# A two-layer hybrid trunk on one core: the framework's scheduler orders the queues by a timeline simulation instead of its default estimates

## The chip, the core and the metric

The kernel runs on one core of a Trainium2 chip. The core has five engines that run their own queues of instructions: TensorE (PE, with its weight loads shown as PEld), VectorE (DVE), ScalarE (ACT), GpSimd (POOL) and SyncE (SP), which here issues all DMAs. An engine takes its instructions strictly in the order of its queue, and an instruction waits on semaphores that other engines or landed DMAs raise. The metric is the device time of one execution in microseconds, from three runs and one profiled execution.

## The reference

A trunk of two layers works on 1024 latent tokens and 256 context tokens of width 1024, in fp32. Each layer modulates its input (adaLN), projects it, mixes it by two groups of heads, gates, projects out, and normalises the residual.

```python
# layer 0
oa = block_attention(qa, concat([ka_c, ka], 1), concat([va_c, va], 1))   # MLA heads
ob = block_attention(qb, concat([kb_c, kb], 1), concat([vb_c, vb], 1))   # GQA heads
y  = concat([oa * silu(ga), ob * silu(gb)], -1) @ w_out
# layer 1, per direction: gated DeltaNet in chunks of 64, and RG-LRU
sol = triangular_solve(I + M, rhs, lower=True, unit_diagonal=True); u, w = split(sol)
v_new = u - w @ s;  o = qd @ s + attn @ v_new;  s = s * gl + kd^T @ v_new     # scan over chunks
h = linear_scan(a, b, h0)                                                      # RG-LRU
# both layers
x = layer_norm(alpha * x + gate * y)
```

## The kernel before, in words

Every fp32 product is made of three matmuls on parts of the operands: a high part in a reduced format and the rest (names ending in h and l: wh/wl, hh/hl, qh/ql). The splits are made by ScalarE, VectorE and GpSimd. Tokens are worked in tiles of 128, and two column ranges of a wide product run in PSUM tiles of 512 columns.

The stages in order of time: modulation and input projection of layer 0 (to about 360 us); attention with its softmax sums, GQA heads first and MLA heads after (to about 880); the output projection and normalisation, tile by tile (to about 1060); the input projection of layer 1 with the RG-LRU's convolutions and scans beside it (to about 1300); the preparation of the DeltaNet (to about 1510), its triangular levels, scan and output projection (to the end).

What matters here of the attention: score matmuls read the query tiles qh and ql, which have two buffers each and are loaded from d_q (lines 683 and 684). While the GQA heads run, the weights of the MLA heads are fetched in pieces into tiles f with three buffers (lines 639 and 652) and split into wukv and wuq by ScalarE and GpSimd. GpSimd also adds the softmax terms (accp).

What matters of the DeltaNet's preparation: for each tile of tokens VectorE writes decayed products into two tiles WX, one for each direction, and SyncE stores them to d_w (line 1758) and d_xa (line 1760). When five tiles are stored, the 32x32 blocks on their diagonals are loaded (line 1785, tiles ia) and inverted by a chain of 30 steps with two instructions each: direction 0 on VectorE, direction 1 on GpSimd. The result is stored to d_bu (line 1802), its transpose (tile it) to d_bt (line 1805):

```python
eng = nc.gpsimd if dr else nc.vector
...
eng.tensor_tensor(tv, A[:, rows, j].unsqueeze(2).broadcast_to([80, nr, ncl]),
                  A[:, j, cols].unsqueeze(1).broadcast_to([80, nr, ncl]), op=ALU.mult)
eng.tensor_tensor(A[:, rows, cols], A[:, rows, cols], tv, op=ALU.add)
...
nc.sync.dma_start(d["bu"][dr, ...], A)
T = self.til(gp, [80, 32, 32], F32, "it", bufs=1)
eng.tensor_copy(T, A.rearrange("p a b -> p b a"))
nc.sync.dma_start(d["bt"][dr, ...], T)
```

There are four inverses: ia_2716 and ia_2816 on VectorE, ia_2717 and ia_2817 on GpSimd. The levels and the scan load W, X, Tt, Tu, K and V (lines 1839 to 1859) from what was stored. Beside the preparation run convolutions (tiles yc), weight splits (wf) and the projections of the gates, whose PSUM tiles are emptied through tiles tm.

Two things set the order of the work. The first is the kernel's own planner (class Core, lines 93 to 110): it counts a cost for every instruction that is emitted and lets generators of background work emit when an engine's count is behind TensorE's. It fixes the order in which the instructions are emitted. The second is the framework's scheduler, which runs when the tile context closes. It gives every engine a queue: of the instructions that its own estimates of time make ready it takes the one emitted first. It also gives tiles their buffers and sets the waits. Almost all compute instructions are recorded with line 88, since they go through one helper; the names of the tiles tell them apart.

## Time and profile before

| | us |
|---|---|
| three timed runs | 1791.7, 1804.87, 1804.99 |
| median | 1804.87 |
| profiled execution | 1793.42 |
| its span, first to last instruction | 1791.6 |
| TensorE busy in it | 1636.8 |
| VectorE, ScalarE, GpSimd busy | 1169.4, 738.1, 798.5 |
| mean granted clock of TensorE, as a share of full speed | 0.957 |
| data moved by DMA | 234.31 MB |

The profile is that of one execution. A row of its timeline gives the start in us from the beginning of the span, the duration in us, engine and line, operation, output and inputs by the program's names, shapes, how many such instructions in a row are put together, and, in brackets, how long the engine stood idle before the row and what it waited for.

### The profile page before, as it was taken

What the parts mean: (1) busy time and instruction counts of PE and PEld (TensorE: products, weight loads), DVE (VectorE), ACT (ScalarE), POOL (GpSimd) and SP (SyncE); (2) the same over time, 40 slices, a digit from 0 to 9 for tenths busy, and PEclk for the clock granted to TensorE, in tenths of its full rate; (3) what the DMA queues carried; (4) which work ended last, traced back from release to release, by engine and by line L of the source; (5) the groups of instructions that cost most, each with busy time, mean ns of one, the idle gap of its engine ahead of it and who ended that gap; (6) DMA issues with size and microseconds to landing.
All of it is one profiled execution on the core that took longest, in us unless ns stands there. A gap on an engine that the chain in (4) does not pass through costs nothing.

```text
span 1791.6 us, 25469 instructions
## 1 busy us (share of the span) xinstructions
PE 1636.8 (91%) x9020; PEld 1196.4 (67%) x9020; DVE 1169.4 (65%) x2186; ACT 738.1 (41%) x1498; POOL 798.5 (45%) x727
## 2 busy tenths in 40 slices
PE   5999999988999999999899989979978958899997
PEld 2997776744555665656467877756855747799885
DVE  2757713235667767666847976998846596477786
ACT  2533401144554554544524445767733312233431
POOL 1432200066657778767642752322204483573120
PEclk8999999998999999999899999989988979899999
DMA  7343396155231101011243323333456637897542
GB/s 304 114 142 118 120 315 202 66 127 157 66 84 48 51 21 47 28 55 54 89 124 105 119 91 118 106 120 121 124 153 167 155 107 219 280 250 229 183 159 94
DMA packets 239931, 234.31 MB, mean 131 GB/s; under 512 B 61958, under 2 KB 188306, under 8 KB 237756
## 3 DMA queue, kind: packets, MB, share of 16 engines
q1 hardware_dynamic: 239804, 232.69, 42.4%
q8 instruction: 71, 1.16, 0.3%
q14 instruction: 56, 0.46, 0.1%
HBM read 162.97 MB, written 69.66 MB: 130 GB/s over the span
## 4 chain that ended last, share of the span: by engine, by line
PE 57%; DVE 18%; issue 7%; DMA 6%; POOL 5%; ACT 4%; SPq 2%; DVEq 0%; ACTq 0%; POOLq 0%
PE ps L88 39%; PE pb L88 10%; PE pv L88 8%; DVE yc L88 3%; DVE f L88 2%; DVE mx L88 1%; DVE ia L88 1%; DVE itmp L88 1%; POOL ia L88 1%; DMA modw<-in_mod_w 1%; POOL itmp L88 1%; DVE nsq L88 1%; DVE lu L88 1%; POOL lu L88 1%; DMA wst<-in_att_w_in 1%
## 5 line engine op out<-in xcount | busy, mean ns | idle before, releaser
L88 DVE TENSOR_REDUCE mx<-ps 128x1 f32<-128x512 f32 (+1 forms) x384 | 206.9, 593 | 161.3 <-PE ps L88 160.2
L88 POOL TENSOR_TENSOR accp<-accp,pt 128x512 f32<-128x512 f32 x202 | 266.1, 1340 | 71.0 <-ACT pt L88 69.4
L88 PE MATMUL ps<-h1h,wf 128*128 128x512 f32 (+1 forms) x864 | 276.7, 394 | 5.7 <-DVE tm L88 3.5
L88 ACT ACTIVATE pt<-pb 128x512 f32<-128x512 f32 (+1 forms) x352 | 194.7, 577 | 194.8 <-PE pb L88 191.1
L88 PE MATMUL pb<-qh,kb 96*128 96x512 f32 (+4 forms) x528 | 209.1, 411 | 1.7 <-ACT pt L88 1.2
L88 PEld LDWEIGHTS ps<-h1h,wf 128*128 128x128 f32 x864 | 164.0, 196 | 41.9 <-issue 5.6
L88 PE MATMUL ps<-h1l,wf 128*128 128x512 f32 (+1 forms) x432 | 164.7, 381 | 0.0
L88 PEld LDWEIGHTS pb<-qh,kb 128*128 128x128 f32 (+2 forms) x528 | 99.9, 191 | 88.9 <-issue 66.2
L88 PE MATMUL pb<-ql,kb 66*128 66x512 f32 (+3 forms) x352 | 136.8, 389 | 0.0
L88 PE MATMUL ps<-kb,qh 128*128 128x512 f32 (+3 forms) x416 | 120.5, 365 | 13.3 <-DMA qh<-d_q 9.7
L88 POOL TENSOR_TENSOR accp<-pt,pt 128x512 f32<-128x512 f32 (+1 forms) x47 | 54.2, 1171 | 140.5 <-ACT pt L88 128.5
L88 PEld LDWEIGHTS ps<-kb,qh 128*128 128x128 f32 (+1 forms) x416 | 75.9, 189 | 48.9 <-DMA qh<-d_q 10.3
L88 DVE SCALAR_TENSOR_TENSOR yc<-xb,rT,yc 128x1283 f32<-128x1283 f32 (+1 forms) x48 | 88.8, 1859 | 26.2 <-ACT yc L88 25.9
L88 POOL TENSOR_TENSOR ml<-m,mh 128x512 fp32r<-128x512 f32 (+1 forms) x24 | 45.5, 1908 | 116.4 <-ACT mh L88 107.1
L88 PEld LDWEIGHTS ps<-h1l,wf 128*128 128x128 f32 x432 | 85.0, 197 | 16.5 <-issue 3.7
L88 PE MATMUL ps<-wl,hh 128*128 128x416 f32 (+2 forms) x240 | 83.6, 348 | 7.6 <-DVE wl L88 3.8
L88 PE MATMUL ps<-wh,hh 128*128 128x416 f32 (+2 forms) x240 | 83.9, 349 | 3.8 <-ACT wh L88 2.7
L88 PE MATMUL pv<-pt,vm 128*64 128x512 f32 (+1 forms) x352 | 83.0, 589 | 4.1 <-DVE mo L88 2.7
L88 PE MATMUL ps<-wo,mh 128*128 128x512 f32 x256 | 83.0, 403 | 2.4 <-ACT wo L88 2.2
L88 PE MATMUL pv<-pt,vgqa 128*64 128x512 f32 (+1 forms) x352 | 84.2, 600 | 1.0 <-DVE mo L88 1.0
L88 PE MATMUL ps<-wh,hl 128*128 128x416 f32 (+2 forms) x240 | 82.7, 345 | 0.1
L88 PE MATMUL ps<-w,mh 128*128 128x512 f32 x256 | 81.3, 398 | 0.0
(373 smaller groups left out, 3679.9 us busy)
## 6 DMA issues: line engine op xcount, KB each, us to landing
modw<-in_mod_w SPq DMA_DIRECT2D x16, 1024.0 KB
wfs<-in_rec_w_in SPq DMA_DIRECT2D x22, 512.0 KB
modw<-in_mod_w SPq DMA_DIRECT2D x16, 512.0 KB
wst<-in_att_w_in SPq DMA_DIRECT2D x24, 256.0 KB
d_q<-qo SPq DMA_DIRECT2D x20, 256.0 KB
lx<-d_xl SPq DMA_DIRECT2D x8, 640.0 KB
d_w<-WX SPq DMA_DIRECT2D x20, 256.0 KB
W<-d_w SPq DMA_DIRECT2D x20, 256.0 KB
```

The costliest lines, as they stand in the source:

```text
L88: return fn(*args, **kw)
```

## The change

One argument is added where the tile context is opened.

```diff
-    with tile.TileContext(nc) as tc:
+    with tile.TileContext(nc, schedule_with_timeline_sim=True) as tc:
         Trunk(tc, I, out).run()
```

The scheduler then takes the times at which instructions become ready from a simulation of the engines' timelines, and no longer from its default estimates. The instructions are emitted as before. Both programs have the same 7592 matmuls and 884 DMAs, and the same compute instructions on the other engines but for 31 loads of ScalarE's function tables instead of 29; only their order in each queue differs, and which buffer a tile gets. No matmul is moved by more than 51 places, and in the attention the orders of TensorE and VectorE are the same.

Place 1 is SyncE's queue at the end of the first half of the GQA heads, with the load of the query tiles qh_807 and ql_808. Before:

```order
L875 DMA d_mix_17_94<-mo_712_3502 128x256
L639 DMA f_773_3688<-in_mla_w_ukv 128x4x64
L639 DMA f_789_3747<-in_mla_w_ukv 128x4x64
L627 DMA mlat_734_3561<-in_k_mla 128x1024
...
L639 DMA f_803_3800<-in_mla_w_ukv 128x4x64
L683 DMA qh_807_3818<-d_q12_12_89 128x4x128
L684 DMA ql_808_3819<-d_q12_12_89 64x4x128
```

and with the change:

```order
L639 DMA f_757_3631<-in_mla_w_ukv 128x4x64
L639 DMA f_773_3688<-in_mla_w_ukv 128x4x64
...
L875 DMA d_mix_17_94<-mo_712_3502 128x256
L639 DMA f_789_3747<-in_mla_w_ukv 128x4x64
L639 DMA f_803_3800<-in_mla_w_ukv 128x4x64
L652 DMA f_824_3859<-in_mla_w_uq 128x4x96
L683 DMA qh_807_3818<-d_q12_12_89 128x4x128
L684 DMA ql_808_3819<-d_q12_12_89 64x4x128
```

The piece f_803 needs the buffer of f_757, which is free when GpSimd has made wukv of it; f_824 needs that of f_773. On GpSimd this first wukv row stands now behind accp of pt_746, 12 places earlier than before, where it stood behind accp of pt_814; the second one follows two rows after it.

Place 2 is SyncE's queue near the end of the DeltaNet's preparation. Before, the store d_bu of GpSimd's first inverse (ia_2717) and that of its transpose stand ahead of the stores of two pairs of WX tiles:

```order
L1760 DMA d_xa_2189_8715<-WX_2766_11988 512x1x128
L1802 DMA d_bu_2191_8717<-ia_2717_11798 80x1024
L1805 DMA d_bt_2190_8716<-it_2840_12356 80x1024
L1572 DMA d_v_2182_8708<-tm_2827_12282 128x4x128
L1758 DMA d_w_2188_8714<-WX_2790_12113 128x4x128
L1760 DMA d_xa_2189_8715<-WX_2790_12113 512x1x128
...
L1758 DMA d_w_2188_8714<-WX_2809_12194 128x4x128
...
L1785 DMA ia_2816_12224<-d_w_2188_8714 20x32x32 x4
L1785 DMA ia_2817_12229<-d_w_2188_8714 20x32x32 x4
```

With the change:

```order
L1758 DMA d_w_2188_8714<-WX_2790_12113 128x4x128
...
L1758 DMA d_w_2188_8714<-WX_2809_12194 128x4x128
L1760 DMA d_xa_2189_8715<-WX_2809_12194 512x1x128
L1758 DMA d_w_2188_8714<-WX_2810_12195 128x4x128
L1760 DMA d_xa_2189_8715<-WX_2810_12195 512x1x128
L1785 DMA ia_2816_12224<-d_w_2188_8714 20x32x32 x4
...
L1802 DMA d_bu_2191_8717<-ia_2717_11798 80x1024
...
L1785 DMA ia_2817_12229<-d_w_2188_8714 20x32x32 x4
L1805 DMA d_bt_2190_8716<-it_2840_12356 80x1024
```

The WX stores and the loads for VectorE's second inverse stand ahead of d_bu now; those for GpSimd's second inverse stay behind it. On VectorE the rows of WX_2809 and WX_2810 follow those of WX_2790 and WX_2791 directly, where one wf row and two yc_2830 rows stood between them. Further on, the row that empties the PSUM tile of the z gate (tm_2873) stood behind 42 rows of the second inverse, and stands behind 11 of them now.

Place 3 is TensorE's queue in the input projection of layer 0, where two PSUM tiles (ps_220 and ps_221) are summed over the pieces of one weight. Before, one after the other:

```order
L88 MATMUL ps_220_970<-wl_205_923,hh_23_106 128x256
L88 MATMUL ps_220_970<-wh_204_922,hl_24_107 128x256
L88 MATMUL ps_221_997<-wh_183_880,hh_23_106 128x256
L88 MATMUL ps_221_997<-wl_184_881,hh_23_106 128x256
L88 MATMUL ps_221_997<-wh_183_880,hl_24_107 128x256
```

With the change, mixed:

```order
L88 MATMUL ps_221_997<-wl_184_881,hh_23_106 128x256
L88 MATMUL ps_221_997<-wh_183_880,hl_24_107 128x256
L88 MATMUL ps_221_997<-wh_186_886,hh_23_106 128x256
L88 MATMUL ps_220_970<-wh_198_910,hh_23_106 128x256
L88 MATMUL ps_221_997<-wl_187_887,hh_23_106 128x256
```

The matmuls of the second tile with the early pieces stand between those of the first tile with the late pieces. The same is done at two more places: with the next weight, and at the end of the attention, where matmuls of the context's output projection (pb_2174, pb_2175) now precede those of the last softmax sum.

## Rows read from the trace of the kernel before

**Rows 1.** The page, part 1: busy us, share of the span, instructions of each engine.

```profile
PE 1636.8 (91%) x9020; PEld 1196.4 (67%) x9020; DVE 1169.4 (65%) x2186; ACT 738.1 (41%) x1498; POOL 798.5 (45%) x727
```

**Rows 2.** Stretches: us, busy PE, PEld, DVE, ACT, POOL (instructions), clock, DMA share, GB/s.

```profile
0.00:50.00 50.00, 30.61 (x152) 15.55 (x153) 15.55 (x34) 13.60 (x27) 8.84 (x14) 0.86 0.82 313
...
1430.00:1515.00 85.00, 61.11 (x281) 49.23 (x280) 72.29 (x139) 19.99 (x43) 51.33 (x75) 0.84 0.55 158
1515.00:1575.00 60.00, 52.16 (x634) 44.16 (x634) 26.53 (x71) 15.28 (x40) 35.74 (x57) 0.89 0.89 274
1575.00:1690.00 115.00, 110.84 (x1400) 102.41 (x1397) 86.77 (x257) 47.09 (x133) 50.63 (x79) 0.99 0.77 231
...
1440.00:1466.00 26.00, 7.70 (x22) 5.32 (x21) 24.97 (x40) 2.36 (x7) 23.33 (x35) 0.55 0.25 59
```

**Rows 3.** Timeline of TensorE, 416 to 433 us.

```profile
416.97 0.40 PE L88 MATMUL pb<-qh,kb 128*128 128x512 f32 x1
...
432.40 0.79 PE L88 MATMUL ps<-kb,qh 128*128 128x512 f32 x1 [8.37 <-DMA qh<-d_q]
```

**Rows 4.** Waits of SyncE's queue, 405-434 and 1385-1420 us: total, times, longest.

```profile
SPq L639 <- POOL wukv L88: 19.1, 1, 19.1
...
SPq L1802 <- POOL ia L88: 15.8, 1, 15.8
```

**Rows 5.** Timeline of SyncE's queue in the same two stretches.

```profile
428.86 0.38 SPq L639 DMA_DIRECT2D f<-in_mla_w_ukv  x1
429.35 0.45 SPq L683 DMA_DIRECT2D qh<-d_q  x1
...
1409.79 0.87 SPq L1758 DMA_DIRECT2D d_w<-WX  x1
```

**Rows 6.** Timeline of VectorE, 1414 to 1501 us.

```profile
1414.40 0.88 DVE L88 SCALAR_TENSOR_TENSOR WX<-ps,g_s,D 128x256 f32<-128x256 f32 x2 [12.26 <-DMA d_xa<-WX]
...
1432.90 0.68 DVE L88 TENSOR_SCALAR ia<-ia 80x1024 f32<-80x1024 f32 x1
...
1499.92 1.13 DVE L88 COPY it<-ia 80x1024 f32<-80x1024 f32 x1
```

**Rows 7.** Timeline of GpSimd, 1430 to 1476 us.

```profile
1430.14 2.77 POOL L88 TENSOR_SCALAR ia<-ia 80x1024 f32<-80x1024 f32 x1 [21.27 <-DMA ia<-d_w]
...
1473.85 2.16 POOL L88 COPY it<-ia 80x1024 f32<-80x1024 f32 x1
```

**Rows 8.** Chain of waits before 1513 us: start, us, what.

```profile
1507.73 5.29 DMA Tt<-d_bt
```

**Rows 9.** Timeline of TensorE, 1457 to 1514 us.

```profile
1457.87 0.69 PE L88 MATMUL ps<-ident,yc 128*128 128x128 f32 x2 [17.35 <-DVE tm L88]
...
1513.11 0.64 PE L88 MATMUL ps<-Tt,W 32*32 32x32 f32 x16 [1.86 <-DMA Tt<-d_bt]
```

**Rows 10.** Timeline of VectorE: two products of the inverse of one size.

```profile
1444.76 0.77 DVE L88 TENSOR_TENSOR itmp<-ia 80x234 f32<-80x234 f32 x1
...
1481.75 0.40 DVE L88 TENSOR_TENSOR itmp<-ia 80x234 f32<-80x234 f32 x1
```

**Rows 11.** Timeline of TensorE: three shorter waits in layer 0.

```profile
102.95 0.39 PE L88 MATMUL ps<-wl,hh 128*128 128x256 f32 x1 [2.42 <-POOL wl L88]
...
145.98 0.79 PE L88 MATMUL ps<-wl,hh 128*128 128x512 f32 x1 [2.95 <-DVE wl L88]
...
885.58 1.16 PE L88 MATMUL pv<-pt,vm 128*64 128x256 f32 x8 [2.71 <-DVE mo L88]
```

**Rows 12.** Timeline of TensorE, first loads of the scan.

```profile
1544.55 3.35 PE L88 MATMUL ps<-V,Lt 128*128 128x128 f32 x16 [3.01 <-DMA V<-d_v]
...
1561.19 0.80 PE L88 MATMUL ps<-K,L 128*128 128x128 f32 x2 [4.62 <-POOL K L88]
```

**Rows 13.** The page, part 5: a group | busy us, mean ns | idle before, releaser.

```profile
L88 DVE SCALAR_TENSOR_TENSOR yc<-xb,rT,yc 128x1283 f32<-128x1283 f32 (+1 forms) x48 | 88.8, 1859 | 26.2 <-ACT yc L88 25.9
```

**Rows 14.** Groups of ScalarE, in the same columns.

```profile
L88 ACT ACT_TABLE_LOAD x29 | 37.2, 1283 | 13.6 <-DVE yc L88 12.4 <-PEq L2229 0.7
```

## The prediction, made before the changed kernel was run

> **What bounds the kernel now.** I read the engine totals first: TensorE is busy 91% of the span [rows 1], so time can only be won where it stands still or where it runs slowly. I then cut the span into stages [rows 2]: in the stage 1430 to 1515 TensorE works 61.11 of 85 us at a granted clock of 0.84 while VectorE works 72.29; in 1515 to 1575 the DMA engines are 89% busy; in 1575 to 1690 TensorE works 110.84 of 115, so hardly anything is to be had there. Last I listed TensorE's waits. The two longest are 8.37 us at 432.40 [rows 3] and 17.35 us at 1457.87 [rows 9]. Neither is a shortage of an engine: behind each, SyncE's queue stands at one DMA whose data is late, while DMAs that are ready stand behind it [rows 4, 5]. The change gives every engine's queue another order, so I followed both programs through these two places and through the smaller waits.
>
> **Base of the sum.** The profiled execution took 1793.42 us (span 1791.6). The timed runs are 1791.7, 1804.87 and 1804.99: two groups 12 us apart, and the trace belongs to the lower. I make the sum against 1793.42 and let the range carry the other group.
>
> **Term 1, the query load at 432: -8 us.** Before, SyncE holds the third mla_w_ukv load group's last piece (L639) until GpSimd has split the first one, a wait of 19.1 us [rows 4], and issues it at 428.86; the query loads (L683, L684) stand behind it and start at 429.35 [rows 5]. TensorE starts with them at 432.40, so a load needs 3.05 us from issue to use. The buffer they fill is read for the last time by the score matmul at 416.97 [rows 3]. In the change GpSimd splits that weight 12 places earlier, among accp sums, so SyncE gets past it and waits for the buffer alone: issue about 417.5, usable about 420.5. TensorE arrives at 432.40 - 8.37 = 424.03, so the wait goes. Late next is nothing that I can see: TensorE's order around it is the same, and 8.3 of 8.37 should stay, since TensorE is what limits the attention stage. Bounds: -8.4, and 0 if another load in front (L652, which now precedes the query loads) is as late as L639 is now. I take -8, since its split is only two GpSimd rows further on.
>
> **Term 2, the inverses at 1390 to 1513: -9 us.** Before, SyncE waits 15.8 us at L1802 for the end of GpSimd's inverse [rows 4], then for its transpose (L1805), and the stores of the ready WX tiles (L1758, L1760) leave only at 1409.79 [rows 5]. The next WX has no buffer until they land: VectorE stands 12.26 us, until 1414.40 [rows 6]. Everything after hangs on that: GpSimd's second inverse starts at 1430.14 after 21.27 us of idling [rows 7], VectorE's at 1432.90, and the latter ends with the copy at 1499.92 [rows 6]; its transposed result is stored, loaded (5.29 us) and only then do TensorE's triangular levels run on, at 1513 [rows 8, 9]. The change puts both pairs of WX stores and the four block loads of VectorE's inverse ahead of L1802, so VectorE need not stand at 1402. It takes one wf subtraction and two yc passes after the WX instead of before, which costs nothing in sum, and then meets the block loads. Now the last of eight pieces is there 1430.14 - 1414.40 = 15.7 us after the first WX row [rows 6, 7]; the four that VectorE needs should be there in two thirds of it, 10 us. Until it needs them it has the WX, some 3 us, and four rows of the yc kind, of 1.86 us or less [rows 13], 7 us. That is nearly even; I leave up to 3 us of new wait: 12.26 - 3 = 9 us gained at the end of its chain, and from there at 1513.
>
> What of TensorE's 17.35 us? It waits for the evacuation tm, which stands on VectorE behind 42 rows of the inverse; in the change 11 rows precede it, so this wait should go, and with it the slow clock behind it: granted 0.55 in 1440 to 1466 [rows 2]. But TensorE then only arrives earlier at the levels, which wait for VectorE's chain. The wait moves there; it is no gain of its own. Bounds: 0 (all given back at 1513) and -20 (the 17.35 and some 2.5 of slow clock, if VectorE's chain were not the end). I take the value that VectorE's row gives.
>
> **Term 3, small fillings: -4 us.** TensorE waits 2.42 us at 102.95 and 2.95 at 145.98 for weight splits, and 2.71 at 885.58 at the last softmax sums [rows 11]. In the change matmuls of another accumulation, whose operands are there, stand in front of the waiting ones. Of the 8.1 us I count half, since the producers (GpSimd and VectorE) set the pace of the following tile too. Bounds: -8.1 and 0.
>
> **Term 4, start: +1 us.** SyncE's queue begins with eight 1 MB modw loads and the context rows; now six weight pieces of 0.2 MB and the rotary tables of 0.26 MB stand among them, 1.5 MB, which at the 313 GB/s of this stage [rows 2] bring the context rows 4.8 us later. TensorE gets the same pieces back as smaller waits for weights, for which it stands now and then up to 50. I take most of it as given back. Bounds: -1, +4.8.
>
> **Term 5, the scan's loads: -2 us.** TensorE waits 3.01 us for V and 4.62 for K [rows 12]. The V loads move ahead of the kk/qq loads, and one w_out load of 256 KB leaves the way of K. Against it three 512 KB broadcasts move from the scan's last third to the crowded stretch. At that stage's 274 GB/s [rows 2] these 1.5 MB are 5.7 us of DMA. Bounds: -7.6, +6.
>
> **Term 6, ScalarE's tables: 0.** 31 instead of 29 loads of 1.283 us [rows 14] are 2.6 us on an engine that is busy 41%. TensorE's nearest matmuls cover it; uncovered it costs 2.6.
>
> **Allowance: +5 us.** 230 of 7592 matmuls and 275 VectorE rows stand elsewhere; new waits can't be read from the old trace. I allow two of the size of those in [rows 11].
>
> Sum: -8 - 9 - 4 + 1 - 2 + 0 + 5 = -17, so 1793.4 - 17 = 1776 us.
>
> **A rule that speaks against term 2.** VectorE's inverse rows are slower while GpSimd's inverse runs: the 80x234 product takes 0.77 us at 1444.76, and 0.40 at 1481.75, after GpSimd's chain has ended [rows 7, 10]. The Trainium skill, "SBUF — State Buffer", section "SBUF: two separate sides", says that VectorE and GpSimd share a port pair as an exclusive lock, which a VectorE operation with two SBUF inputs and a GpSimd operation can't hold together, so one blocks. The trace agrees with it in those two rows; carried as far as in rival (a) it makes the time 1783 instead of 1776.
>
> **Rivals.**
> (a) *The two inverses hinder each other more.* GpSimd's chain lasts from 1430.14 to 1476.0, 46 us; each of them costs VectorE 1 - 0.40/0.77 = 0.48 us of work. If more VectorE work of other kinds falls opposite it and stretches it by a third, 15 us, VectorE loses 7 and term 2 is -2: 1783. For it: both chains slide together, with yc passes now between the inverse's rows. Against it: the work displaced then runs after GpSimd's end, at 0.40. Chance 0.18.
> (b) *TensorE's wait is itself the path.* If the levels' loads come early enough, term 2 is -20: 1765. Against it: the chain of waits runs over VectorE's copy and the Tt load. Chance 0.12.
> (c) *Slower: the scan's loads fall behind.* Ten steps from 1540 to 1690 each need K, X and V from one queue. If in the new order a load that waits for a buffer (w_out's wait for VectorE's split of the one before) stands in front of them, a K comes late in each step by about 3 us, the V wait of [rows 12]: 10 x 3 = 30 us, and 1776 + 2 + 30 = 1808, later than before. It decides where a K lands after the state of the step before is done, for which TensorE's 4 us of slack in 1575 to 1690 is the measure [rows 2]. Against it: for every step the K and V loads have the same buffer wait as before and follow it at once. Chance 0.08.
> (d) *It does not do what the orders show:* SyncE is held at both places by some other late operand, and the rest cancels: 1793. Chance 0.12.
> The forecast keeps 0.50.
>
> **How the numbers follow.** The forecast's own range, from the bounds of its terms, is 1766 to 1787 (the bounds of terms 1 to 5 don't all come together). Rivals (a) and (b) lie in it or at its edge. If the runs fall in the upper group it is 1777 to 1798. The range 1760 to 1799 takes these in with most of (d), and leaves out (c). The median before is 1804.87, and 1% (about what a measurement can tell) is 18 us: below 1786.8 counts as faster. In the lower group the forecast, (b) and most of (a) are, in the upper one (b) and half of the forecast; like against like the gain is just under 1%. I give faster 0.50, same 0.43, slower 0.07, the last for (c) and what I can't see.
>
> **What would show it.** Right: no wait of TensorE over 1 us near 424 and the L683 issue at about 417; SyncE's wait for GpSimd's inverse no longer in front of a WX store, and no VectorE wait of 12 us near 1400; the tm evacuation less than 2 us after TensorE needs it; a TensorE wait for Tt of over 10 us that has taken its place; the Tt matmuls of 1513 at about 1493 (-8 - 9 - 4 + 1). Wrong: inverse rows on VectorE at 0.7 us and more over most of the chain (a); waits for K or X over 2 us in several steps of the scan (c); a new SyncE wait over 10 us with query or WX DMAs behind it (d).

## The result, and the profile after

The changed kernel takes **1790.35 us** (median of ten runs, 1785.47 to 1794.67). The kernel before, in ten runs, takes 1800.31 us (1791.70 to 1804.99). The ratio is 0.994 with a 95% interval of 0.9921 to 0.9959: about 10 us faster, which is clear of the noise and less than the 1% from which on the forecast counted a change as faster. The forecast was 17 us faster and 1776 us. Of the 14 us between 1776 and 1790, 7 are the base: the ten runs of before don't form two groups, as I had read the three that I saw, and the profiled execution of 1793.42 lies 6.9 us under their median. The other 7 are the effect itself, and the rest of this text is about them. (One of the five runs of s5_both_back below took 1941.35 us at a granted clock of 0.786; its ratio leaves it out.)

The profiled execution after took 1786.52 us, its span is 1784.7. The totals that answer to [rows 1]:

```profile
PE 1630.5 (91%) x9020; PEld 1195.9 (67%) x9020; DVE 1177.7 (66%) x2186; ACT 741.0 (42%) x1500; POOL 811.2 (45%) x727
```

TensorE is 6.3 us less busy with the same matmuls (less of it at the slow clock), VectorE 8.3 and GpSimd 12.7 us busier with the same instructions. So the rows of these two engines take longer in sum; one such row is followed below.

**The query load.** SyncE's queue and then TensorE, timeline, at the place of [rows 3, 5] (columns: start, length, engine, line, operation, and in brackets the idle time before it with what ended it):

```profile
406.05 4.93 SPq L652 DMA_DIRECT2D f<-in_mla_w_uq  x1
414.70 0.37 SPq L683 DMA_DIRECT2D qh<-d_q  x1
```

```profile
422.06 0.51 PE L88 MATMUL ps<-kb,qh 128*128 128x512 f32 x1
```

The load leaves at 414.70 instead of 429.35, and the score matmul that waited 8.37 us starts at 422.06 without a bracket, so without a wait. L652, which now stands in front of the load, is through at 410.98; after it the load waits 3.9 us more for its buffer, which TensorE still reads.

**The inverses.** Their places of [rows 4 to 10]: SyncE, VectorE and TensorE after the change.

```profile
1394.40 0.37 SPq L1758 DMA_DIRECT2D d_w<-WX  x1
1396.81 3.43 SPq L1785 DMA_DIRECT2D ia<-d_w  x4
1408.85 0.33 SPq L1802 DMA_DIRECT2D d_bu<-ia  x1
```

```profile
1389.94 0.88 DVE L88 SCALAR_TENSOR_TENSOR WX<-ps,g_s,D 128x256 f32<-128x256 f32 x2 [2.98 <-DMA d_xa<-WX]
1392.32 2.44 DVE L88 SCALAR_TENSOR_TENSOR WX<-ps,g_s,D 128x256 f32<-128x256 f32 x6 [1.50 <-DMA d_xa<-WX]
...
1402.53 0.69 DVE L88 TENSOR_SCALAR ia<-ia 80x1024 f32<-80x1024 f32 x1 [1.36 <-DMA ia<-d_w]
...
1422.59 0.39 DVE L88 TENSOR_TENSOR itmp<-ia 80x234 f32<-80x234 f32 x1
...
1486.15 1.03 DVE L88 COPY it<-ia 80x1024 f32<-80x1024 f32 x1
```

```profile
1497.16 0.64 PE L88 MATMUL ps<-Tt,W 32*32 32x32 f32 x16 [19.50 <-DMA Tt<-d_bt]
```

The WX stores and the block loads now leave ahead of the store of GpSimd's inverse (L1802, 1408.85). In place of one wait of 12.26 us VectorE has three of 2.98, 1.50 and 1.36. Its inverse starts 30.4 us earlier (1402.53 for 1432.90) and its copy 13.8 us earlier (1486.15 for 1499.92), since yc, wf and tm rows now stand between its rows. TensorE's 17.35 us for tm [rows 9] are gone and 19.50 us for Tt have come.

**Where the time went.** For each stage between two fixed matmuls I took TensorE's time in every trace of this study, those of the experiments too: "old" are the traces in which that stage has the orders of before, "new" those with the change's orders (the experiments say which). s1, s2 and s5 are left out of the stages whose old orders they put back; their figures stand with them. The experiments ran in three batches on three chips. In most stages the traces of one order agree far better than whole runs do.

```text
stage (clock of before)        old: mean (lowest-highest, traces)   new: mean                    new - old
   0- 410 start                413.0 (410.2-417.1, 5)               408.0 (403.9-411.0, 9)       -5.0
 410- 447 query load            37.9 ( 37.2- 38.7, 2)                28.8 ( 28.1- 30.2, 7)       -9.1
 447- 584                      137.0 (136.1-138.4, 7)               136.1 (135.7-136.5, 5)       -0.9
 584- 640                       56.5 ( 56.5- 56.5, 7)                62.6 ( 61.7- 63.3, 4)       +6.1
 640- 880                      240.3 (240.3-240.4, 7)               241.4 (240.8-243.0, 5)       +1.1
 880- 961 attention's end       80.7 ( 79.5- 82.1, 7)                86.1 ( 84.2- 88.1, 5)       +5.3
 961-1057                       99.2 ( 99.2- 99.3, 7)                98.5 ( 98.4- 98.6, 5)       -0.7
1057-1300 LRU                  240.0 (239.5-240.7, 7)               244.1 (243.2-245.2, 5)       +4.1
1300-1513 inverses             214.9 (212.5-219.0, 3)               199.5 (198.0-201.9, 6)      -15.4
1513-1690 scan                 176.1 (175.7-176.8, 3)               176.4 (174.5-177.9, 6)       +0.3
1690-end                       100.4 ( 99.1-101.6, 7)               107.3 (106.9-108.0, 6)       +7.0
```

The gains are 5.0 + 9.1 + 0.9 + 0.7 + 15.4 = 31 us, the losses 6.1 + 1.1 + 5.3 + 4.1 + 0.3 + 7.0 = 24 us. So the two places on which the forecast rests gave more than it said, and other places took most of it back. In the two profiled executions alone the same account gives -6.9, which is the difference of their spans.

One cut of this table is badly placed: around the matmul at 1690 the two orders mix the scan's matmuls with those of the output in different ways. From the matmul at 1702.56 on TensorE's orders agree. Cut there, the stage from 1513 takes 188.1 us (3 old traces) and 191.2 (6 new ones), and the rest 89.1 (the same in 7 old traces) and 92.5 (92.2 to 93.0 in 6). So only 3.4 of the 7.0 us are the tail's; some 3 belong to the scan.

**The places.** On VectorE at 584 one product of 32x512 takes 4.71 us; its like in the kernel before takes 0.68. That row of before, then the rows of VectorE and of GpSimd around the long one after the change (timeline):

```profile
596.18 0.68 DVE L88 TENSOR_TENSOR f<-f,f 32x512 f32<-32x512 f32 x1
```

```profile
583.56 0.69 DVE L88 TENSOR_TENSOR f<-ps,mlat 32x512 f32<-32x512 f32 x1 [0.44 <-POOL ql L88]
584.28 4.71 DVE L88 TENSOR_TENSOR f<-f,f 32x512 f32<-32x512 f32 x1
589.02 3.30 DVE L88 TENSOR_REDUCE mx<-ps 128x1 f32<-128x512 f32 x6
```

```profile
582.80 1.96 POOL L88 TENSOR_TENSOR ql<-f,qh 96x256 fp32r<-96x256 f32 x2 [1.16 <-ACT qh L88]
584.72 2.51 POOL L88 TENSOR_TENSOR accp<-pt,pt 128x512 f32<-128x512 f32 x2
587.19 1.26 POOL L88 TENSOR_TENSOR accp<-accp,pt 128x512 f32<-128x512 f32 x1
589.73 1.28 POOL L88 TENSOR_TENSOR ql<-f,qh 96x512 fp32r<-96x512 f32 x1 [1.29 <-ACT qh L88]
```

VectorE's product runs until 588.99; GpSimd's five instructions follow each other without a gap from 582.80 to 588.45. The maxima that stand behind it are what TensorE then waits for, 3.27 us, and from 590.80 to 594.20 it works at a granted clock of 0.50. That wait, and those at the end of the attention and in the LRU, on TensorE:

```profile
589.77 1.09 PE L88 MATMUL ps<-kb,qh 96*128 96x512 f32 x2 [3.27 <-DVE mx L88]
...
920.31 0.64 PE L88 MATMUL ps<-accp,ones 128*64 128x512 f32 x1
...
939.05 2.08 PE L88 MATMUL ps<-w,mh 128*128 128x512 f32 x4 [3.36 <-ACT mh L88]
...
1102.07 6.23 PE L88 MATMUL ps<-lx,gw 128*128 128x256 f32 x12 [3.71 <-DMA gw<-in_lru_gate_w]
...
1140.58 2.04 PE L88 MATMUL ps<-lx,gw 128*128 128x256 f32 x4 [4.36 <-DMA lx<-d_xl]
```

At 920.31 are the last softmax sums, behind 40 projection matmuls, 33 more than before; the wait for mh (the high part of the attention's gated output) at 939.05 hangs on those sums, and a granted clock of 0.50 follows it until 945.8. At 1102.07 and 1140.58 weights of the LRU's gates (gw) and its input (lx) are late. On VectorE the scan of one unit now stands behind three rows of the next unit (the last two are shown), and on SyncE its store (L1503), behind which the input's load stands in both kernels, waits for it:

```profile
1123.82 3.04 DVE L88 TENSOR_SCALAR lv<-lv 128x1280 f32<-128x1280 f32 x1
1126.78 1.48 DVE L88 SCALAR_TENSOR_TENSOR lx<-lw,lv 128x1280 f32<-128x1280 f32 x1
1128.18 2.81 DVE L88 TENSOR_TENSOR_SCAN lw<-lv,lu 128x1280 f32<-128x1280 f32 x1
```

```profile
1131.02 0.33 SPq L1503 DMA_DIRECT2D d_hs<-lw  x1
...
1136.49 0.32 SPq L1457 DMA_DIRECT2D lx<-d_xl  x1
```

In the kernel before, the scan started at 1119.37, the store left at 1122.23 and the load at 1130.82:

```profile
1119.37 2.83 DVE L88 TENSOR_TENSOR_SCAN lw<-lv,lu 128x1280 f32<-128x1280 f32 x1
```

Of the 8.8 us by which the scan is later, 2.8 were there ahead of the three rows: VectorE waits for a product of GpSimd (lu) until 1119.69, before until 1116.92.

In the scan of the DeltaNet, TensorE waits 3.28 us for a row qs of VectorE, which now stands behind two longer rows (zt and S) that it preceded before:

```profile
1645.77 0.69 DVE L88 TENSOR_TENSOR qs<-qs,rs_r 128x512 f32<-128x512 f32 x1
```

```profile
1646.61 1.08 PE L88 MATMUL ps<-ident,qs 128*128 128x128 f32 x4 [3.28 <-DVE qs L88]
```

In the kernel before this wait is 0.54 us (at 1655.49). A wait of 3.27 or 3.28 us stands there in all six traces with the change's orders, and none over 1.9 us in the other eight. Last, VectorE at the end of the span:

```profile
1770.14 1.22 DVE L88 TENSOR_TENSOR x<-x,bcln_b 128x1024 f32<-128x1024 f32 x1
1771.28 0.68 DVE L88 TENSOR_TENSOR r<-ps,gl 128x512 f32<-128x512 f32 x1
```

TensorE's last matmul ends at 1768.45. The last tile's first product (r) starts 2.8 us later, since two passes of the tile before (the second is the row at 1770.14) stand in front of it. In the kernel before it starts while the last matmuls still run (1778.17, last matmul at 1778.43):

```profile
1778.17 0.69 DVE L88 TENSOR_TENSOR r<-ps,gl 128x512 f32<-128x512 f32 x1 [1.37 <-PE ps L88]
```

From TensorE's end to the end of the span it takes 16.3 us, before 12.8: these are the tail's 3.4.

### The profile page after: what moved, and what is told of

It reads as the page before. It is cut to its first block, busy times and chain, and to the rows that moved or that the text cites. A ratio compares the mean times of both kernels' runs of the same rounds, so it can differ in the third digit from the quotient of the medians.

```text
span 1784.7 us, 25505 instructions
## 1 busy us (share of the span) xinstructions
PE 1630.5 (91%) x9020; PEld 1195.9 (67%) x9020; DVE 1177.7 (66%) x2186; ACT 741.0 (42%) x1500; POOL 811.2 (45%) x727
## 4 chain that ended last, share of the span: by engine, by line
PE 51%; DVE 18%; DMA 13%; issue 7%; ACT 6%; POOL 3%; SPq 2%; ACTq 0%; DVEq 0%; POOLq 0%
PE ps L88 34%; PE pb L88 10%; PE pv L88 7%; DMA wst<-in_att_w_in 2%; DVE f L88 2%; DMA wh<-in_rec_w_out 2%; DVE x L88 2%; DVE yc L88 2%; DVE lw L88 1%; DVE mx L88 1%; DMA qh<-d_q 1%; DMA d_xa<-WX 1%; DVE WX L88 1%; DVE r L88 1%; DVE lu L88 1%
## 5 line engine op out<-in xcount | busy, mean ns | idle before, releaser
L88 PE MATMUL ps<-h1h,wf 128*128 128x512 f32 (+1 forms) x864 | 270.5, 388 | 3.5 <-DVE tm L88 1.6
L88 PEld LDWEIGHTS ps<-kb,qh 128*128 128x128 f32 (+1 forms) x416 | 76.9, 191 | 44.8 <-DVE mx L88 12.8
L88 POOL TENSOR_TENSOR ml<-m,mh 128x512 fp32r<-128x512 f32 (+1 forms) x24 | 52.6, 2205 | 114.0 <-ACT mh L88 114.0
L88 DVE SCALAR_TENSOR_TENSOR yc<-xb,rT,yc 128x1283 f32<-128x1283 f32 (+1 forms) x48 | 84.1, 1759 | 24.5 <-ACT yc L88 24.1
L88 PEld LDWEIGHTS ps<-h1l,wf 128*128 128x128 f32 x432 | 83.9, 194 | 16.6 <-issue 3.6
L88 PE MATMUL ps<-wl,hh 128*128 128x416 f32 (+2 forms) x240 | 81.5, 342 | 0.0
```

The costliest lines, as they stand in the source:

```text
L88: return fn(*args, **kw)
```

## The experiments

Two kinds of edit were made. The first kind changes the kernel before so that it gets one of the forecast's terms alone. The second holds the order of every engine fixed by a table and gives one stretch of the program the order of before, or of the change. No run holds the change's orders fixed with nothing altered; s4, in which two GpSimd rows are moved, comes closest, and its stages elsewhere lie in the ranges of the new orders. Their core is the same in all of them (the table PINS lists, engine by engine, the numbers of the instructions as the program emits them):

```diff
+def pin(tc):
+    byname = {i.name: i for i in tc.nc.cur_bb.bb.instructions}
+    for line in PINS:
...
+        for p, q in zip(names, names[1:]):
+            tc.add_manual_dep(byname[q], p, mybir.DependencyInfo(mybir.DependencyClass.NoSync, mybir.DependencyReason.DATA))
...
+        pin(tc)
```

Medians of before were 1799.81 us beside the first four kernels, 1804.48 beside s1 to s4, and 1799.19 beside r9, r10, s5 and s6, so the ratios are what is compared.

### e1_query: term 1 alone

The last mla_w_ukv piece gets a buffer of its own, so SyncE need not wait for GpSimd's split before it.

```diff
-                    st = self.til(ap, [P, 512], F32, "f", bufs=3)
+                    st = self.til(ap, [P, 256], F32, "fw", bufs=1) if h * e else self.til(ap, [P, 512], F32, "f", bufs=3)
```

> The kernel before with one thing changed: the fourth load of the mla_w_ukv pieces has a buffer of its own (1 KB a partition), so SyncE no longer holds the query loads behind it; the orders of TensorE and VectorE stay as before, word for word. Theory A (the prediction's term 1: TensorE limits the attention, what it no longer waits for stays won): the TensorE wait of 8.37 us at 432 is gone, everything behind it is 8 us earlier to the end, 8 us under the kernel before. Theory B (the gain is real at 432, but the stages from 940 on hang on chains of VectorE, GpSimd and loads that swallow it): -8 at 440 and at 900, less than 3 of it left at 1320 and at the end. Theory C (a VectorE stall like the 4.71 us one of the change at 584 comes whenever the attention slides): -8 at 440, -3 at 620.

Measured: 1793.58 us, ratio 0.9966 (0.9947 to 0.9984). On SyncE and on TensorE:

```profile
417.93 0.37 SPq L683 DMA_DIRECT2D qh<-d_q  x1
```

```profile
425.52 0.50 PE L88 MATMUL ps<-kb,qh 128*128 128x512 f32 x1 [0.96 <-DMA qh<-d_q]
...
1309.60 1.02 PE L88 MATMUL ps<-dec 16*128 16x512 f32 x2 [7.33 <-DMA dec<-d_dec]
```

The wait falls from 8.37 to 0.96 us and TensorE is 5 to 6 us ahead all the way to 1300, so term 1 is real and nothing in the attention takes it back. From 1300 to 1340 this trace then loses 6.1 us (46.2 for 40.1). The wait for dec (the decay rows) is 1.3 us longer than in before, and the clock stays low for much longer behind it. Stretches of the trace of e1_query (length; busy PE, PEld, DVE, ACT, POOL; granted clock; DMA share; GB/s), from the wait on, and then those of before:

```profile
1304.50:1309.60 5.10, 0.01 (x1) 0.01 (x1) 1.74 (x1) 0.00 (x0) 0.38 (x1) 0.65 0.66 168
1309.60:1319.70 10.10, 9.64 (x30) 6.85 (x31) 6.60 (x15) 4.89 (x14) 0.00 (x0) 0.50 0.40 105
1319.70:1333.00 13.30, 12.84 (x32) 8.52 (x32) 4.38 (x12) 2.71 (x11) 0.00 (x0) 0.50 0.45 125
```

```profile
1315.00:1325.10 10.10, 9.98 (x32) 6.66 (x32) 6.60 (x15) 4.97 (x14) 0.00 (x0) 0.59 0.41 104
1325.10:1333.00 7.90, 7.30 (x33) 5.14 (x32) 2.39 (x6) 2.71 (x11) 0.00 (x0) 1.00 0.61 159
```

### e2_stores: term 2 alone

In the kernel before, the two stores of GpSimd's first inverse are put behind the block loads of VectorE's second one.

```diff
+            block = nc.sync.dma_start(A[q::4], ...)
+        if (dr, b) == (0, 1):
+            self.block = block
...
+        for x in (bu, bt) if (dr, b) == (1, 0) else ():
+            self.tc.add_manual_dep(x.ins, self.block.ins.name, mybir.DependencyInfo(mybir.DependencyClass.NoSync, mybir.DependencyReason.DATA))
```

> The kernel before, with the two stores of GpSimd's first inverse (L1802, L1805) held behind the last WX stores and the block loads of VectorE's inverse in SyncE's order; VectorE still does its yc passes ahead of its inverse. Theory A (the prediction's term 2): VectorE's 12.26 us stand at 1414 is gone or under 3 us, VectorE's inverse and the levels of 1513 come 9 us earlier, and the time is 9 us less. Rival (a) of the prediction (the two inverses hinder each other): -2. Theory D (the change's gain of 12 us in this stage came from the VectorE inverse that starts ahead of the yc passes, not from the stores alone): the inverse starts some 10 us earlier here against 30 us in the change, and the levels come 5 us or less earlier.

Measured: 1789.19 us, ratio 0.9939 (0.9919 to 0.9959). VectorE and TensorE:

```profile
1410.85 3.21 DVE L88 SCALAR_TENSOR_TENSOR WX<-ps,g_s,D 128x256 f32<-128x256 f32 x8
```

```profile
1461.30 0.80 PE L88 MATMUL ps<-h1h,wf 128*128 128x512 f32 x1 [13.64 <-DVE tm L88]
```

The stage 1300 to 1513 falls from 213.2 to 199.8 us, as low as with the change (198.0 to 201.9), although TensorE's wait for tm still stands there with 13.64 us. The WX rows that waited 12.26 us start at 1410.85 without a wait. So the gain of the inverses comes when no store of an unfinished inverse stands in front of stores that are ready, and rival (b), in which TensorE's own wait is the path, falls. The edit isn't quite alone: with the stores held back the scheduler also moves rows on other engines behind this place (56 of VectorE and 37 of ScalarE between 1434 and 1630), and no run holds those still.

### e3_both: both terms, nothing else

The two edits together.

```diff
+ (the edit of e1_query)
+ (the edit of e2_stores)
```

> The kernel before with both edits: the query loads freed and the stores of GpSimd's inverse held back. If the two gains are independent and both stay (theory A): -17, faster than the change by 7 to 10 us. If the first is swallowed behind 940 (theory B): the same as the second edit alone, -9. If the second is bounded by VectorE's order (theory D): -8 to -13.

Measured: 1783.02 us, ratio 0.9903 (0.9874 to 0.9931), -17 us. Two edits in the kernel before give the forecast's 17. That is 7 us more than the change itself, with intervals that overlap (0.9921 to 0.9959 there); by the medians the rest of the change's new order is a loss in sum.

### e4_sums: the sums at the attention's end

In the changed kernel, the region of hand-written order is to reach over the first projection, so that the projection can't stand in front of the last sums.

```diff
-        order.close()
         self.split(mh1, ml1, m, "a", "v")
...
         self.out_mm(self.y0[0], mh, ml, self.wo, range(KT))
+        order.close()
```

> The changed kernel with one thing undone: at the end of the attention TensorE does the last softmax sums (ps<-accp and ps<-accv) ahead of the first output-projection tile's matmuls, as they were emitted, where the change did 17 projection matmuls first. My theory (the projection matmuls in front put the sums 4 to 5 us back, the chain sums, reciprocal, store, load, mh then ends where it did before, and TensorE waits 3.36 us for mh with a slow clock behind it): sums near 916.5 instead of 920.3, mh near 934 instead of 938, no TensorE wait at 939 and no slow clock, TensorE 4 to 7 us earlier at 960 than in the change. Rival (the mh load hangs on something else than the sums): nothing moves at 960. At the end: 4 us less than the change if the stages behind don't swallow it, 0 if they do.

Measured: 1792.70 us, ratio 0.996 (0.9942 to 0.9978). A miss of the edit: the matmuls that stand in front of the sums belong to the second projection, outside the region, so no row moved. What it gives is a second trace of the change's order: 62.2 us from 584 to 640 and 86.8 from 880 to 961, so both losses belong to the order and not to one execution.

### s1_attention: the old orders from 447 to 961

The change's orders everywhere, but in the attention's stretch (instructions 5200 to 8880 as emitted) those of before on every engine.

```diff
+PINS = (... the change's orders, 5200-8880 as before ...)
+        pin(tc)
```

> The changed kernel with the engine orders of the kernel before put back in one stretch of the emission, from the sixth attention unit (trace time 575) to the start of the second layer norm (960), and the change's own orders pinned everywhere else. My theory (the change loses there what it won at 432: a VectorE row of 0.68 us that takes 4.71 us behind GpSimd's back-to-back sums at 584, and 17 projection matmuls ahead of the last softmax sums at 914): TensorE needs 56.5 us instead of 62 between the places that lie at 584 and 640 in the kernel before, and 81 instead of 85 to 87 between 880 and 961, so it is 9 to 11 us earlier at 961 than in the change; if that stays to the end, the time is 9 us under the change. Rival (the stages behind hang on other chains): 9 us earlier at 961 and less than 3 at the end.

Measured: 1780.81 us, ratio 0.9875 (0.9847 to 0.9904), 0.0065 under the change's, some 12 us. From 584 to 640 it takes 57.1 us, from 880 to 961 81.8. The sums and mh stand earlier (TensorE, ScalarE):

```profile
911.58 0.64 PE L88 MATMUL ps<-accp,ones 128*64 128x512 f32 x1
```

```profile
928.72 1.06 ACT L88 ACTIVATE mh<-m 128x1024 fp32r<-128x1024 f32 x1 [20.02 <-DMA m<-d_mix]
```

In the changed kernel they stand at 920.31 and 937.95, with TensorE only 1.2 us later at 905. So the attention loses some 12 us by the medians, and by the stages 62.6 - 57.1 = 5.5 and 86.1 - 81.8 = 4.3, some 10; term 1 is kept without them.

### s2_lru: the old orders from 1057 to 1300

```diff
+PINS = (... the change's orders, 9700-11400 as before ...)
+        pin(tc)
```

> The changed kernel with the engine orders of the kernel before put back in the stretch of the LRU stage (trace time 1060 to 1300) alone. My theory (the change's orders of VectorE and SyncE there cost TensorE two waits, 3.71 us for gate weights at 1102 and 4.36 us for the scan's input at 1140, with a slow clock behind each): between the places of 1090 and 1137 TensorE needs 47 to 50 us instead of 56 to 57, some of it given back by 1300, 3 to 4 us less at 1300 and at the end. Rival (TensorE only waits there for what it had won before, and the chain behind is the same in both orders): 0 at 1300.

Measured: 1787.81 us, ratio 0.9913 (0.9881 to 0.9945). The stage is back at 240.6 us, its waits for gw and lx fall (between 1064 and 1140 TensorE's longest is now 1.41 us, for lx at 1105.85), and the attention's losses stay (63.3 and 84.2). The time is 0.0027 under the change's, 5 us, with intervals that overlap: the 4 us of the stage are shown, in the whole time they are at the edge.

### s3_start: e3 with the change's start

The kernel of e3_both, with the change's orders for instructions 0 to 1600 alone.

```diff
+PINS = (... the orders of e3_both, 0-1600 as in the change ...)
+        pin(tc)
```

> The kernel before with both SyncE edits (query loads freed, inverse stores held back; 17 us under the kernel before) and, on top, the change's engine orders in the stretch of the emission from the start to trace time 160. The change needed 101.4 us from 51 to 160 where four runs of the old orders needed 109 to 113. If those orders are the cause and what they win stays: 8 us earlier at 160 and 5 to 8 us less at the end, 1775 to 1778. Rival (the next stage, 160 to 245, hangs on weight splits that are no earlier): 8 us at 160, 3 or less at 245, no difference at the end.

Measured: **1769.77 us, ratio 0.9821 (0.9787 to 0.9855)**, about 32 us faster than before and 21 faster than the change, so it beats both. The stretch 51 to 160 takes 102.0 us here and 101.2 to 102.2 in all nine traces with this start, against 109.0 to 113.2 with the old one; the stretches up to 410 give some of it back (the account above: -5.0). By the ratios the start is worth 15 us with an interval of about 8; the traces say 5. Which is nearer I can't tell: the trace of s3_start is that of its run of 1777.68 us, 8 above its median, that of e3_both of 1775.06, 8 below its own, and the two ran on different chips.

### s4_pool_rows: GpSimd's rows at 584

The change's orders, with GpSimd's rows behind the first two ql splits in the order of before (GpSimd's rows in turn, the change's and this kernel's).

```diff
-accp<-pt,pt  accp<-pt,pt  accp<-accp,pt  ql<-f,qh  accp<-accp,pt  ql<-f,qh
+ql<-f,qh  accp<-pt,pt  ql<-f,qh  accp<-pt,pt  accp<-accp,pt  accp<-accp,pt
```

> The changed kernel with five GpSimd rows put back into the order of the kernel before, at trace time 584: the query split waits between the softmax sums again, so that GpSimd's sums don't follow each other without a gap; every other row of every engine as in the change. Theory of the port (VectorE's row with two SBUF operands can't start while GpSimd's rows follow each other without a gap): the 4.71 us row takes 0.7 to 1.5 us, and TensorE needs 56.5 to 58 us from 584 to 640 instead of 62; 4 to 5 us less at 640. Rival (the row waits for ScalarE's order, which is not changed here): 4.71 and 62 stay.

Measured: 1785.75 us, ratio 0.9902 (0.9867 to 0.9937), 0.0038 or 7 us under the change's, with intervals that overlap. VectorE's product and GpSimd beside it:

```profile
588.00 1.02 DVE L88 TENSOR_TENSOR f<-f,f 32x512 f32<-32x512 f32 x1
```

```profile
586.51 1.96 POOL L88 TENSOR_TENSOR ql<-f,qh 96x256 fp32r<-96x256 f32 x2 [1.16 <-ACT qh L88]
591.20 0.73 POOL L88 TENSOR_TENSOR ql<-f,qh 96x256 fp32r<-96x256 f32 x1 [2.73 <-ACT qh L88]
```

Behind the two ql splits GpSimd now has 2.73 us without work, and the product takes 1.02 us instead of 4.71. The stage takes 56.3 us, as before, and the granted clock stays at 1.00. The orders of VectorE, ScalarE and SyncE are those of the change. So the whole loss of 6.1 us at 584 comes from what GpSimd has beside one VectorE instruction. That VectorE's product waits for GpSimd is the rule that the prediction drew from the Trainium skill, "SBUF — State Buffer", section "SBUF: two separate sides"; the trace agrees that one blocks the other, but the 4.71 us go over the ends of several GpSimd instructions, where the page speaks of the whole of one.

### s5_both_back: s1 and s2 together

```diff
+PINS = (... the change's orders, 5200-8880 and 9700-11400 as before ...)
+        pin(tc)
```

> The changed kernel with the orders of the kernel before put back in both stretches, the attention from 575 to 960 and the LRU stage from 1060 to 1300. If the two losses are separate and all of the gap between the forecast and the change: the change's 10 us, and 12 and 4 more, about 26 us under the kernel before. If the LRU stage swallows what the attention wins (rival): no more than the attention stretch alone gave, 22.

Measured: 1775.32 us, ratio 0.9853 (0.9825 to 0.9881), -26 us. That is the sum of two separate losses, but the interval, 21 to 32 us, takes in the rival's 22 too. In the trace both stretches are won: 81.5 us from 880 to 961 and 240.0 from 1057 to 1300.

### s6_tail_back: everything from 1300 on as in e3

```diff
+PINS = (... the change's orders up to 11400, then those of e3_both ...)
+        pin(tc)
```

> The changed kernel up to trace time 1300, and from there the orders of the kernel with both SyncE edits: the change's orders for the inverses, the scan and the output against mine. In the profile of the change VectorE does the last-but-one output tile's two passes ahead of the last tile's rows (TensorE's end to the end of the span 16.3 us instead of 12.8), and TensorE needs 41.8 us instead of 37.4 to 38.6 between the places of 1690 and 1730. Theory (these orders lose what the change won at the inverses): 5 to 8 us less than the change. Rival (the two orders are worth the same from 1300 on, the differences by place are shifts of work): within 2 us of the change.

Measured: 1786.67 us, ratio 0.9933 (0.9911 to 0.9956), not to be told from the change. In its trace the tail is back: 101.0 us from 1690 to the end, and VectorE's last tile again starts as soon as TensorE's sum for it is there:

```profile
1772.09 1.23 DVE L88 TENSOR_TENSOR x<-x,bcln_b 128x1024 f32<-128x1024 f32 x1
1774.68 0.69 DVE L88 TENSOR_TENSOR r<-ps,gl 128x512 f32<-128x512 f32 x1 [1.37 <-PE ps L88]
```

From 1300 to the end it takes 478.5 us against 481.4 to 486.0 in the six traces with the change's orders there. That is 3 to 7.5 us in the traces that the medians don't show. The 7 us are a loss of that stage; that they are a loss of the whole is not shown.

### r9_dec_queue and r10_best_dec: the wait for dec

Half of the small stores of dec go through ScalarE's queue: in the kernel of e1_query (its orders held fixed) for r9, in that of s3_start for r10.

```diff
-                nc.sync.dma_start(self.d["dec"][:, 4 * h + 2:4 * h + 4, P * h:P * h + P], r[h::4, 2:4])
+                nc.scalar.dma_start(self.d["dec"][:, 4 * h + 2:4 * h + 4, P * h:P * h + P], r[h::4, 2:4])
```

> The kernel with the query loads freed (the run of the query edit alone, whose TensorE was 5.4 us ahead at 1315 and 0.9 us behind at 1340), with one thing more: four of the eight stores of the decay rows go through ScalarE's DMA queue instead of SyncE's; every other row as in that run. There TensorE waited 7.33 us for the decay rows instead of 6.00, and the granted clock stood at 0.5 for 27.3 us behind it instead of 10.2. Theory (the query edit's gain is lost there to the slow clock behind a wait that is only 1.3 us longer): four issues of 0.78 us less in front of the load bring the wait to about 4.2 us, the slow stretch behind it is 10 us or less, TensorE needs 38 to 40 us instead of 46 between the places of 1300 and 1340, and the time is 5 to 8 us less than with the query edit alone. Rival (the landing of the stores, not their issue, is what the load waits for): 7 us and 46 us stay.

> The fastest kernel so far (both SyncE edits and the change's orders up to trace time 160; 32 us under the kernel before), with four of the eight stores of the decay rows on ScalarE's DMA queue. It too needed 46.1 us from 1300 to 1340 with a 27.3 us stretch at clock 0.5. Theory of the slow clock: 38 to 40 there, 6 us less at the end if the inverse stage doesn't swallow it, about 1764. Rival (the stage behind hangs on GpSimd's inverse, not on TensorE): 6 us at 1340, none at 1513 and at the end.

Measured: r9 1791.11 us, ratio 0.9952 (0.9933 to 0.9971); r10 1769.66 us, ratio 0.9833 (0.9807 to 0.9859). TensorE's wait in r9:

```profile
1318.13 1.07 PE L88 MATMUL ps<-dec 16*128 16x512 f32 x2 [3.31 <-DMA dec<-d_dec]
```

The wait falls from 7.33 to 3.31 us and the stretch 1300 to 1340 from 46.2 to 37.7; in r10 from 46.1 to 40.9. At the end neither is to be told from its parent (0.9966, 0.9821), where 5 to 8 us were forecast for r9. The stretch's loss in e1 is thus due to that wait and the slow clock behind it (in one trace of each), but removing it buys nothing that the medians show. s3_start stays the one to take: r10 is no faster.

## Why the prediction was half right

**Two steps failed, the allowance and the base. The allowance:** "I allow two of the size of those in [rows 11]", +5 us. The new waits and stretched rows come to 24 us by the account above: 6.1 at 584, 1.1 up to 880, 5.3 at the attention's end, 4.1 in the LRU, 7.3 in the scan and the tail. (That the last are lost in the whole time too is not shown, by s6.) 230 matmuls and 275 VectorE rows stand elsewhere, and I put a round number on them instead of reading them. s1, s2 and s4 show the attention's, the LRU's and the GpSimd rows' part as separate costs. The two orders held all these places: five GpSimd instructions in a row beside VectorE's chain, projection matmuls in front of the sums for which mh waits (I had booked those under term 3 as a gain), a scan behind rows of the next unit, zt and S in front of a qs row, two passes of one tile in front of the next tile's first row.

**Term 1, -8:** right, -9.1 in the stage, and e1 alone keeps 5 to 6 us of it to 1300. "Late next is nothing that I can see" holds at the place itself: 0.96 us of wait are left in e1, none in the change. The L683 issue came at 414.70 (forecast about 417).

**Term 2, -9:** the mechanism was right and the size too small, -15.4 (e2 alone: -13.4 against before). I had counted one wait of VectorE, 12.26 us less 3. The stretch from 1380 to the end of VectorE's copy (length; busy PE, PEld, DVE, ACT, POOL; granted clock; DMA share; GB/s), before and after:

```profile
1380.00:1501.05 121.05, 101.11 (x440) 81.11 (x441) 91.46 (x168) 34.70 (x74) 73.49 (x109) 0.88 0.52 146
```

```profile
1380.00:1487.18 107.18, 96.69 (x450) 79.16 (x448) 94.18 (x166) 33.02 (x72) 75.97 (x108) 0.97 0.53 153
```

VectorE was idle for 121.05 - 91.46 = 29.6 us and is now for 107.18 - 94.18 = 13.0: 16.6 us less, for 2.7 us more of work. The smaller waits around the 12.26 went too, and yc rows that had stood by themselves now stand between the inverse's rows. It is the idle time of the whole stretch on the engine that sets its end that I should have summed. The order of the two ends was right: TensorE's wait moved from tm (17.35) to Tt (19.50), and the Tt matmul of 1513.11 stands at 1500.08 (the first of them at 1497.16), forecast about 1493: at 1300 the change was not ahead at all, 1301.7 for 1300.0, with 11 us forecast.

**Term 3 and term 4, -4 and +1:** together -5.0 at 410 by the means of 5 and 9 traces, though at 885 the filling turned into the loss at the attention's end. In the waits' own places: those at 102.95 and 145.98 are gone, one of 2.89 us at 150.45 has come.

**Term 5, -2:** +0.3 in the table, and with the cut at 1702.56, where the orders agree, +3.1 (188.1 to 191.2), with the new wait of 3.28 us for qs in it. The wait for V fell from 3.01 to 0.61 us, that for K rose from 4.62 to 6.26. **Term 6, 0:** 31 table loads, and nothing shows them.

**The rivals.** (a) is out as priced, since term 2 won 15.4 us and not 2, but what it says happens. The 80x234 product takes 0.39 us at 1422.59, before GpSimd's steps of its second inverse begin at 1423.98, and 0.80 at 1440.91, while they run. The products of VectorE's inverse sum to 53.6 us, before to 51.1: 2.5 us more, where (a) priced 7. The same rule struck where I had not looked, at 584. (b) is out by e2. (c) is out: behind the first K no step of the scan waits for a K, X or V for more than the 0.15 us from which on the trace lists a wait. (d) is out at both places; but its second half, that "the rest cancels", is what happened to most of the gain.

**The base,** the second failing step. I read three runs as two groups and put the profiled execution into the lower. Ten runs show one spread of 13 us, with the median 6.9 us over the profile.

The chances of 0.50 for faster by over 1% and 0.43 for the same rested on that reading too: like against like I had written "just under 1%", and that was the better guide.

## What to carry to other kernels

Ask of a new order not only which long waits go, but which instructions stand in front of the ones that something waits for: on GpSimd beside VectorE's chain, on TensorE in front of sums that a softmax hangs on, on a DMA queue behind a store whose data is late. When a scheduler gives both gains and losses, take the gains alone: two edits and one stretch of its order (s3_start) gave 32 us where the whole order gave 10. Account by stages between fixed matmuls over several traces, and cut where the orders agree: most stages agree to within 0.1 to 4 us where whole runs of one kernel differ by 13.

## What the runs showed of the hardware that I had not expected

- One VectorE product stood for 4.71 us beside GpSimd instructions that followed each other without a gap, past the start of two more rows (584.72, 587.19), and ended 0.54 us after GpSimd paused at 588.45; with a pause at 588.47 in s4 it took 1.02 us, and in before, where GpSimd pauses at 596.24, 0.68. In the inverses, where GpSimd's rows of 0.6 to 0.7 us leave some 0.07 us between them, VectorE's products of that size take 0.6 to 0.8 us instead of 0.4 (1434 to 1463); beside one long GpSimd copy of 2.13 us (1466.95) a product takes 2.17 (1467.16). Yet beside its row TENSOR_SCALAR of 3.27 us (1420.62) products take 0.31 to 1.03. At 584 the hindrance lasted as long as GpSimd's work without a gap; which rows of GpSimd hinder, and when, these runs don't tell.
- The slow clock behind the wait for dec is not told by the wait. In e1 TensorE waits 7.33 us and the granted clock is 0.50 for 23 us after it; in before it waits 6.00 us and is back at 1.00 after 10 us; in the change it waits 7.74 us, and the two stretches from 1316.50 on are granted as follows:

```profile
1316.50:1326.50 10.00, 9.95 (x45) 8.06 (x45) 6.90 (x17) 5.17 (x15) 0.00 (x0) 0.76 0.66 168
1326.50:1334.00 7.50, 7.50 (x33) 5.74 (x33) 4.17 (x11) 2.56 (x10) 0.00 (x0) 1.00 0.54 153
```

  TensorE is at work in all of them (9.95 of 10.00 here, 9.64 of 10.10 and 12.84 of 13.30 in e1), so what keeps the clock at half in e1 stays open.
- The same orders reach the matmul at 410 anywhere from 410.2 to 417.1 us in five executions, while stages such as 584 to 640 repeat to 0.1 us. It isn't the first 51 us, where the DMA engines are 82% busy [rows 2]: these take 50.9 to 51.7. The stretch from 51 to 160 takes 109.0 to 113.2, that from 245 to 410 takes 162.6 to 167.1. What makes them differ, and whether the 13 us between whole runs come from there, is not shown.
